# A decoder block on one core: the first half's projection without the norm's factor, its differences, squares and gate in other places

## The chip, the cores and the metric

The kernel runs on one core of a Trainium2 chip. The metric is the device time of one execution in microseconds (us). In the texts PE is TensorE (matmuls), ACT is ScalarE, DVE is VectorE, POOL is GpSimd and SP is SyncE, from whose queue all loads and stores are issued. Each engine runs its own instructions in a fixed order, and waits when an operand or a buffer is not ready.

## What is computed

One layer on x of 2048 positions by 1024 channels. The parts that matter here:

```python
h = rmsnorm(x, norm1_g[l])          # y = x * rsqrt(mean(x*x) + eps), times g
proj = h @ w_in[l]
p_q, p_k, p_v, p_g, p_a, c_b, c_c, c_h = jnp.split(proj, splits, axis=-1)
q, k, v = p_q * 64 ** -0.5, p_k, p_v              # 4 heads
log_a = jax.nn.log_sigmoid(p_a @ w_gate_up[l] + b_gate[l]) / 16
o = gla_chunked(q, k, v, log_a)                   # chunks, state carried on
o = rmsnorm(o, gla_norm_g[l]) * jax.nn.silu(p_g)
u = c_c * c_h
o_conv = c_b * causal_depthwise_conv(u, conv_w[l])
x = x + jnp.concatenate([o, o_conv], axis=-1) @ w_out[l]
h2 = rmsnorm(x, norm2_g[l])
x = x + (silu(h2 @ w_ffn_gate[l]) * (h2 @ w_ffn_up[l])) @ w_ffn_down[l]
return rmsnorm(x, norm_f_g)
```

The norm's factor rsqrt(mean(x*x) + eps) is one number for each position. It commutes with the projection, so proj is the same number times (x * g) @ w_in.

## The kernel before

The positions are worked on in two halves of 1024, each half as two column blocks j of 512. Channels lie on the 128 partitions, in 8 tiles k for each j. Products are made in fp32r with operands split into a high and a low half: split (L152) lets ACT write the high half and DVE the difference, and a product of 128 channels takes three matmuls (high by high, high by low, low by high; product_step, L386).

The input projection of a half is 12 units u = 0 to 11 (in_proj, L626): k and q (0, 1), v (2, 3), the swish gate (4, 5), then twice c_c, c_h, c_b (6 to 8, 9 to 11). A unit's weights are four quarters of 128x512. Units 2 to 11 are made by seven products in Strassen's manner (PRODUCTS, L34) with weight sums S1 to S4 made on POOL (L374 to L381) and input differences T1 to T4; each of the seven is 12 matmuls. The products accumulate in PSUM banks named mm; some are copied by ACT (c11, c22, c12; L413) before a later product goes on in the same bank, others are added by DVE (L417). Units 0 and 1 of the first half are made without differences, with 96 matmuls each.

The first half starts like this. first_loads (L496) brings rows of x, the first unit's weight quarters (raw) and the transposed input tiles (h). ACT squares the rows (L494), rows_rstd (L479) makes the factor and spreads it over the partitions by four transposes on PE (L488). build_first (L288) then multiplies each input tile by norm weight and factor on DVE (L520), splits it, and issues its six matmuls (L312 to L314). The differences T1, T2, T3 on POOL (L325) are issued behind that, T4 behind unit 1.

The other work is in generators that a tick, after each product, moves on by a step (background, L205; every tick while hurry is set): the gate's weights, the row statistics of the second half, gate (L577: a_ps from the projection's 16 columns, then for four parts z, and in forget_gate Abs, Exp, Ln on ACT and a running sum on DVE), and h1_ahead (L546), which prepares the second half's operands and stores them (si). gla_half (L680) joins after unit 5. The order in which each engine gets its instructions is then made by the program's scheduler, which may put later work first; issue_after holds an instruction behind a given one on the same engine. ACT's function tables are loaded where the order of its functions needs it (ACT_TABLE_LOAD).

Of the kernel before, what the change touches and what calls it, by code (L numbers as in the profile page):

```python
# [51 lines left out]
def tile_hymba_block(ctx, tc, x, xt, win, wa, wgu, wout, wffn, wdown, wdown_first, small, out):  # L52
# [97 lines left out]
    last_hi, raw_loads = [], []  # L150

    def split(src, hi, lo):  # L152
        last_hi[:] = [act.activation(hi, src, AF.Copy)]  # L153
        return dve.tensor_tensor(lo, src, hi.bitcast(F32), ALU.subtract)  # L154
# [71 lines left out]

    def pause(n):
        for _ in range(n):
            yield
# [58 lines left out]
    def build_first(quad, w):  # L288
# [3 lines left out]
        h, o = {}, {}  # L292
        quarters = ("A11", "A12"), ("A21", "A22")
        los = []
        for j in range(2):
            for r in range(2):
                o[r, j] = bank()
            for k in range(KD):
                with ExitStack() as stack:
                    if len(los) > 1:  # L300
                        stack.enter_context(tc.issue_after(los[-2].ins))
                    h[k, j] = quad(k, j)
# [12 lines left out]
            if j == 0:  # L315
                rbs[1] = rows_rstd(squares[1])

        def differences(wanted):
            for n, y, a, b in (
                ("T1", (0, 0), (0, 1), (0, 0)), ("T2", (0, 0), (4, 1), (0, 0)),  # L320
                ("T3", (0, 1), (4, 1), (0, 1)), ("T4", (0, 0), (4, 0), (0, 0)),
            ):
                for k in range(4 if n in wanted else 0):
                    yy, aa, bb = [h[k + dk, j] for dk, j in (y, a, b)]
                    pool.tensor_tensor(yy[:], aa[:], bb[:], ALU.subtract)  # L325
                    ops[n].append(split_op(yy[:]))

        return ops, [(r, j, o[r, j], True) for j in range(2) for r in range(2)], differences

    def plain_unit(src, ops):  # L330

        raw = raw_weights(src)
# [14 lines left out]
    def weight_quarter(src):  # L347
# [10 lines left out]
        split(src, h[:, 0, :], h[:, 1, :])  # L358
        return h
# [35 lines left out]
    def unit(src, ops, into=None, raw=None, onto=None):  # L395
# [13 lines left out]
        def copied(name, o, at):  # L409
# [3 lines left out]
            act.activation(t[:], o[:], AF.Copy)  # L413
# [43 lines left out]
    def row_stats(b):  # L457
# [11 lines left out]
        for t in range(PT):  # L469
# [3 lines left out]
            for e, xn in enumerate(xs):  # L473
                act.activation(xn[:], xn[:], AF.Square, accum_out=ssq[:, t, e : e + 1])
# [4 lines left out]
    def rows_rstd(ssq):  # L479

        v, l, y0 = [mtiny.tile([P, PT], F32, name=n, tag=n) for n in ("msq", "rl", "ry")]
# [9 lines left out]
    rbs, raws, first_weights, last_load, rows, squares = {}, {}, {}, [], {}, {}  # L491
# [4 lines left out]
    def first_loads():  # L496

        raw = rawp.tile([P, 4, PB], F32, name="raw", tag="raw")
        for b in range(2):
# [6 lines left out]
            for k in range(KD):  # L506
                if b == 0 and k % 4 == 0:
                    for i in ((0, 3), (1, 2))[k // 4]:
                        raw_loads.append(load(raw[:, i, :], win[0][:, i, :]))
                h = bt("h") if b else tt("h")  # L510
                raws[b, k] = h
                last_load[:] = [load(h[:], xt[b, :, k, :])]
        for t in range(PT):
            row_squares(0, t)
        rbs[0] = rows_rstd(squares[0])
        for n, i in (("A11", 0), ("A21", 3), ("A12", 1), ("A22", 2)):
            first_weights[n] = weight_quarter(raw[:, i, :])
# [20 lines left out]
    def build_h():  # L538


        def quad(k, j):
            return scaled(col(C_G1 + k), rbs[j], raws[j, k])

        return build_first(quad, first_weights)
# [32 lines left out]
    def gate(half, ops):  # L577
# [15 lines left out]
        act.activation(a_sb[:], a[:], AF.Copy)  # L593
# [32 lines left out]
    def in_proj(half, ops, first=None, differences=None):  # L626
        def units():
            for u in range(12):
# [7 lines left out]
                if half == 0 and u == 1:  # L636
                    del ops["B12"]
                    differences(("T4",))
# [664 lines left out]
```

## Time and profile before

| | us |
|---|---|
| median of 3 runs (range) | 2085.23 (2084.04 to 2087.19) |
| the profiled execution | 2085.32 |
| its span, first to last instruction | 2083.6 |
| PE busy in the span | 2026.7 (97%) |
| DVE, ACT, POOL busy | 1429.0, 965.2, 882.6 |

The span is counted from the first instruction; all starts are from there. In a timeline a line has start and duration in us, engine, line of the kernel, operation, what is written and read, and in brackets the idle time before and what ended it. A matmul's duration there runs longer than its share, since matmuls overlap; the step between two starts tells the pace. A line of waits has the waiting engine, what it waited for, the total in us, how many times, and the longest.

### The profile page before, as it was taken

How to read it: one execution, taken by the hardware profiler on the slowest of the kernel's cores; microseconds unless marked ns; L12 is line 12 of the kernel's file. 1: busy time of each engine (PE TensorE's matmuls, PEld its weight loads, DVE VectorE, ACT ScalarE, POOL GpSimd, SP SyncE). 2: the span in 40 equal slices, each digit the busy share in tenths (PEclk: the TensorE clock that was granted, in tenths of full speed). 3: DMA queues.
4: the chain of work that ended last, by engine and by line, in shares of the span. 5: the costliest groups of instructions: out<-in, count | busy, mean ns of one | idle time of the engine just before them, and what ended most of it. 6: DMA issues, size and time to landing. Idle time of an engine off the chain costs nothing.

```text
span 2083.6 us, 26960 instructions
## 1 busy us (share of the span) xinstructions
PE 2026.7 (97%) x9175; PEld 1651.2 (79%) x9175; DVE 1429.0 (69%) x2057; ACT 965.2 (46%) x1918; POOL 882.6 (42%) x642
## 2 busy tenths in 40 slices
PE   5999999999999999999999999999999999999997
PEld 4778888887888887778888878887888888878886
DVE  7669786549754696787887566654776776666665
ACT  6455455656543245554555442223455444443234
POOL 3427322222102364555555434533655534534545
PEclk9999999999999999999999999999999999999999
DMA  7349495424586882654654587689454465398763
GB/s 277 126 152 313 145 342 160 152 96 137 182 304 206 331 295 96 234 218 175 237 222 163 211 344 275 237 328 361 167 185 159 177 227 202 136 354 318 288 263 121
DMA packets 190395, 464.45 MB, mean 223 GB/s; under 512 B 19952, under 2 KB 67248, under 8 KB 180656
## 3 DMA queue, kind: packets, MB, share of 16 engines
q1 hardware_dynamic: 190256, 462.72, 61.5%
q8 instruction: 72, 1.18, 0.2%
q14 instruction: 67, 0.55, 0.1%
HBM read 297.49 MB, written 165.15 MB: 222 GB/s over the span
## 4 chain that ended last, share of the span: by engine, by line
PE 79%; DVE 6%; DMA 3%; issue 2%; POOL 1%; ACT 1%; SPq 0%; DVEq 0%; POOLq 0%; ACTq 0%
PE mm L391 23%; PE mm L393 23%; PE mm L392 22%; PE mm L824 3%; PE mm L825 2%; PE mm L827 2%; DVE wq L154 2%; DVE so L154 1%; DMA raw<-in_wffn_dram 1%; DMA shT<-so 1%; PE o_ps L748 1%; PE o_ps L750 1%; DMA op<-sa_T 1%; PE sc L724 0%; POOL t L927 0%
## 5 line engine op out<-in xcount | busy, mean ns | idle before, releaser
L391 PE MATMUL mm<-op,wq 128*128 128x512 f32 x2511 | 982.1, 393 | 10.8 <-ACT c L413 5.0
L392 PE MATMUL mm<-op,wq 128*128 128x512 f32 x2511 | 977.3, 389 | 0.0
L393 PE MATMUL mm<-op,wq 128*128 128x512 f32 x2511 | 964.8, 390 | 10.4 <-DVE wq L154 10.2
L154 DVE TENSOR_TENSOR wq<-raw,wq 128x512 fp32r<-128x512 f32 (+2 forms) x626 | 503.0, 810 | 230.7 <-ACT wq L153 228.6
L153 ACT ACTIVATE wq<-raw 128x512 fp32r<-128x512 f32 (+2 forms) x626 | 363.8, 587 | 590.2 <-PE mm L393 456.2
L391 PEld LDWEIGHTS mm<-op,wq 128*128 128x128 f32 x2511 | 472.4, 188 | 122.7 <-ACT c L413 8.6
L393 PEld LDWEIGHTS mm<-op,wq 128*128 128x128 f32 x2511 | 472.5, 188 | 116.7 <-DVE wq L154 18.8
L392 PEld LDWEIGHTS mm<-op,wq 128*128 128x128 f32 x2511 | 472.7, 188 | 96.4 <-issue 1.2
L376 POOL TENSOR_TENSOR raw<-s,raw 128x512 f32<-128x512 f32 (+2 forms) x97 | 127.1, 1310 | 473.4 <-DVE wq L154 446.9
L417 DVE TENSOR_TENSOR y<-mm,y 128x512 f32<-128x512 f32 x185 | 127.2, 689 | 131.5 <-PE mm L393 131.2
L374 POOL TENSOR_TENSOR s<-raw 128x512 f32<-128x512 f32 (+2 forms) x97 | 128.0, 1320 | 205.3 <-DMA raw<-in_wffn_dram 101.4
L381 POOL TENSOR_TENSOR raw<-raw 128x512 f32<-128x512 f32 (+2 forms) x97 | 124.9, 1288 | 164.7 <-DVE wq L154 157.6
L417 DVE TENSOR_TENSOR c<-mm,c 128x512 f32<-128x512 f32 x198 | 135.3, 683 | 64.9 <-PE mm L393 63.6
L806 POOL TENSOR_TENSOR ssx<-ssx,q 128x512 f32<-128x512 f32 x52 | 76.1, 1478 | 161.6 <-ACT q L805 161.5
L375 POOL TENSOR_TENSOR raw<-raw 128x512 f32<-128x512 f32 (+2 forms) x97 | 135.8, 1400 | 5.3
L413 ACT ACTIVATE c<-mm 128x512 f32<-128x512 f32 x198 | 114.9, 587 | 17.3 <-PE mm L393 15.8
L154 DVE TENSOR_TENSOR so<-t,so 128x512 fp32r<-128x512 f32 x100 | 89.1, 896 | 25.2 <-ACT so L153 24.7
L153 ACT ACTIVATE wq<-s 128x512 fp32r<-128x512 f32 (+2 forms) x97 | 56.7, 585 | 95.9 <-PE mm L393 89.0
L824 PE MATMUL mm<-op,wq 128*128 128x512 f32 x256 | 100.9, 395 | 0.0
L825 PE MATMUL mm<-op,wq 128*128 128x512 f32 x256 | 99.8, 390 | 0.0
L154 DVE TENSOR_TENSOR wq<-s,wq 128x512 fp32r<-128x512 f32 (+2 forms) x97 | 81.1, 836 | 9.8 <-ACT wq L153 9.2
L153 ACT ACTIVATE so<-t 128x512 fp32r<-128x512 f32 x100 | 62.5, 627 | 41.6 <-DMA sa_B<-so 17.8
(188 smaller groups left out, 1847.9 us busy)
## 6 DMA issues: line engine op xcount, KB each, us to landing
raw<-in_wffn_dram SPq DMA_DIRECT2D x44, 1024.0 KB, 5.6
sa_T<-so SPq DMA_DIRECT2D x88, 512.0 KB, 5.3
op<-sa_T SPq DMA_DIRECT2D x88, 512.0 KB, 9.6
sa_B<-so SPq DMA_DIRECT2D x69, 512.0 KB, 3.4
op<-sa_B SPq DMA_DIRECT2D x69, 512.0 KB, 9.6
raw<-in_win_dram SPq DMA_DIRECT2D x23, 1024.0 KB, 5.5
raw<-in_wdown_dram SPq DMA_DIRECT2D x24, 768.0 KB, 6.2
sx<-y SPq DMA_DIRECT2D x48, 256.0 KB, 3.0
```

The lines of the kernel that those rows point to most:

```text
L153: last_hi[:] = [act.activation(hi, src, AF.Copy)]
L154: return dve.tensor_tensor(lo, src, hi.bitcast(F32), ALU.subtract)
L374: pool.tensor_tensor(s1, a21, a22, ALU.add)
L375: pool.tensor_tensor(a21, a11, a21, ALU.subtract)
L376: pool.tensor_tensor(a11, s1, a11, ALU.subtract)
L381: pool.tensor_tensor(a12, a12, a11, ALU.subtract)
L391: pe.matmul(o[:, s], wh, xh, start=first and k == 0, stop=False, skip_group_check=True)
L392: pe.matmul(o[:, s], wh, xl, start=False, stop=False, skip_group_check=True)
L393: return pe.matmul(o[:, s], wl, xh, start=False, stop=k == n - 1, skip_group_check=True)
L417: dve.tensor_tensor(t[:], o[:], t[:], ALU.add)
L824: pe.matmul(o[e, j][:], wh, m[:, 0, :], start=k == 0, stop=False)
L825: pe.matmul(o[e, j][:], wh, m[:, 1, :], start=False, stop=False)
```

## The change

The first half's operands are now the input times the norm's weight alone. ACT writes the high half of that product (scale=g), DVE the low half in one scalar_tensor_tensor, and POOL writes the product itself back to h for the differences. Unit 0's weights come by quarters in between, and the loads of weights and input tiles come ahead of the rows of x. The factor is made later, in the background (first_factors), and is put in behind the projection: on v as its square at the positions (positions), on the head norm, on the swish gate, on c_c as its square (factors2) and on the convolution's result by products on POOL (on DVE for the bank still in PSUM), and on the gate's 16 columns. opening issues T1, T2, T3 and the eight row squares at ticks of unit 1. 18 small matmuls on ones stand at PE's start. The gate's generator stands behind the row statistics and eight steps of h1.

```diff
+                g = col(C_G1 + k)
+                if j == 0 and k in (0, 3, 4):
+                    turn(*{0: ("A11", 0), 3: ("A12", 1), 4: ("A22", 2)}[k])
                 x = opp.tile([P, 2, PB], F32R, name="op", tag="op")
-                los.append(split(h[k, j][:], x[:, 0, :], x[:, 1, :]))
-                if j == 0 and k >= PT:
-                    row_squares(1, k - PT)
+                with tc.issue_after(order[-1].ins):
+                    order.append(act.activation(x[:, 0, :], h[k, j][:], AF.Copy, scale=g))
+                if (k, j) == (0, 0):
+                    turn("A21", 3)
+                dve.scalar_tensor_tensor(
+                    x[:, 1, :], h[k, j][:], g, x[:, 0, :].bitcast(F32), ALU.mult, ALU.subtract
+                )
+                pool.tensor_scalar(h[k, j][:], h[k, j][:], g, 1.0, ALU.mult, ALU.mult)
...
+    def opening(differences):
+        def some_squares(b, t):
+            with tc.issue_after(last_weight[0].ins):
+                row_squares(b, t)
+                row_squares(b, t + 1)
+
+        differences("T1", range(4))
+        some_squares(0, 0)
+        yield
+        some_squares(0, 2)
+        yield
+        for i in range(2):
+            differences("T2", range(2 * i, 2 * i + 2))
+            yield
+        for i in range(2):
+            some_squares(1, 2 * i)
+            differences("T3", range(2 * i, 2 * i + 2))
+            yield
+        yield from pause(2)
+
+    def first_factors():
+        for b in range(2):
...
+            with tc.issue_after(last_lo[0].ins):
+                act.activation(factors[b][:], rows_rstd(squares[b], f)[:], AF.Copy)
+                dve.tensor_tensor(f2[:], f[:], f[:], ALU.mult)
...
+    def factored(c, in_psum, f):
+
+        s = tt("n") if in_psum else c
+        (dve if in_psum else pool).tensor_tensor(s[:], c[:], f[:], ALU.mult)
+        return s
...
-        act.activation(a_sb[:], a[:], AF.Copy)
+        if half:
+            act.activation(a_sb[:], a[:], AF.Copy)
+        else:
+            for j in range(2):
+                r = slice(32 * j, 32 * j + 32)
+                dve.tensor_tensor(a_sb[r, :], a[r, :], factors[j][r, :], ALU.mult)
...
+                if half == 0 and u in (4, 5, 6, 9):
+                    c, p = factored(c, p, f[j]), False
...
+                    if half == 0:
+                        pool.tensor_tensor(y[:], y[:], factors[j][:], ALU.mult)
...
+            act.activation(v[:], v_ps[:], AF.Copy, scale=positions[b][1][:, t : t + 1])
...
+    warm = bank("warm")
+    for _ in range(18):
+        pe.matmul(warm[:, 0:P], ones[:], ones[:], start=True, stop=True)
     act.preload_act_table_set("natural_log_exp_and_others")
-    first_loads()
+    raw, second = first_loads()
...
     background.extend(
         [
-            gate_weights(), pause(9), row_stats(2), row_stats(3), gate(0, ops), unhurried(),
-            h1_ahead(),
+            opening(differences), gate_weights(), first_factors(), pause(3), row_stats(2),
+            row_stats(3), begun(h1, 8), gate(0, ops), unhurried(), h1,
         ]
     )
```

Three places of the new order follow. The first is DVE at the start of the program, from its first weight split on; first as it was before (msq, rl are the factor's small tiles, rb_ps its spread in PSUM, wq weights, op operands, h input tiles).

```order
L482 TENSOR_SCALAR msq<-ssq 128x4
L154 TENSOR_TENSOR wq<-raw,wq 128x512 x2
L163 TENSOR_TENSOR rl<-ry 128x4
L164 SCALAR_TENSOR_TENSOR rl<-rl,msq 128x4
L165 SCALAR_TENSOR_TENSOR msq<-rl,ry 128x4
L487 COPY rep<-msq 128x128 x4
L520 SCALAR_TENSOR_TENSOR h<-h,sml,rb_ps 128x512 x2
```

The same place of DVE in the changed order (L320 is the new low half).

```order
L154 TENSOR_TENSOR wq<-raw,wq 128x512
L320 SCALAR_TENSOR_TENSOR op<-h,sml,op 128x512
L154 TENSOR_TENSOR wq<-raw,wq 128x512
L320 SCALAR_TENSOR_TENSOR op<-h,sml,op 128x512 x2
L154 TENSOR_TENSOR wq<-raw,wq 128x512
L320 SCALAR_TENSOR_TENSOR op<-h,sml,op 128x512
L154 TENSOR_TENSOR wq<-raw,wq 128x512
```

The factor's operations are gone from there, and low halves of operands (20 operations for 16 tiles and four quarters) take their place. The second place is POOL right behind its constants, in the changed order; before, the differences L325 were its first work there.

```order
L323 TENSOR_SCALAR h<-h,sml 128x512 x10
L341 TENSOR_TENSOR h<-h 128x512
L323 TENSOR_SCALAR h<-h,sml 128x512
L341 TENSOR_TENSOR h<-h 128x512
L323 TENSOR_SCALAR h<-h,sml 128x512 x3
L341 TENSOR_TENSOR h<-h 128x512
L323 TENSOR_SCALAR h<-h,sml 128x512 x2
L341 TENSOR_TENSOR h<-h 128x512 x5
L391 TENSOR_TENSOR s_935<-raw 128x512
L341 TENSOR_TENSOR h<-h 128x512 x4
```

POOL now has a product for each input tile, with T1 between; s_935 is the weight sum s1 of unit 2, ahead of T2. The third place is ACT in the gate. Before, with the tiles g1 of the gate's parts, between unit 3 and 4:

```order
L442 ACTIVATE c11_1375<-mm_1149 128x512
L153 ACTIVATE wq_1393<-raw_1378 128x512
L610 ACTIVATE g1_1356<-z_1354,sml_99 128x512
L612 ACTIVATE g1_1356<-g1_1356 128x512
L613 ACTIVATE g1_1356<-g1_1356,ones_92 128x512
L153 ACTIVATE wq_1396<-raw_1378 128x512
L413 ACTIVATE c11_1437<-mm_1406 128x512
L610 ACTIVATE g1_1421<-z_1419,sml_99 128x512
L620 ACTIVATE em_1351<-g1_1356 128x4
L612 ACTIVATE g1_1421<-g1_1421 128x512
L613 ACTIVATE g1_1421<-g1_1421,ones_92 128x512
```

In the changed order the gate stands between unit 5 (raw_1531, c22_1590, c12_1613) and unit 6 (raw_1780, bank mm_1808). L660 is Abs, L662 Exp, L663 Ln, L469 silu.

```order
L469 ACTIVATE c22_1590<-c22_1590 128x512
L660 ACTIVATE g1_1682<-z_1680,sml_99 128x512
L153 ACTIVATE wq_1792<-raw_1780 128x512
L662 ACT_TABLE_LOAD
L662 ACTIVATE g1_1682<-g1_1682 128x512
L660 ACTIVATE g1_1713<-z_1711,sml_99 128x512
L663 ACT_TABLE_LOAD
L663 ACTIVATE g1_1682<-g1_1682,ones_92 128x512
L662 ACT_TABLE_LOAD
L662 ACTIVATE g1_1713<-g1_1713 128x512
L660 ACTIVATE g1_1747<-z_1745,sml_99 128x512
L469 ACT_TABLE_LOAD
```

It goes on from there (em and el are small results of the gate, wq_1795 and wq_1798 weights A12 and S3 of unit 6):

```order
L663 ACT_TABLE_LOAD
L663 ACTIVATE g1_1713<-g1_1713,ones_92 128x512
L662 ACT_TABLE_LOAD
L662 ACTIVATE g1_1747<-g1_1747 128x512
L670 ACTIVATE em_1677<-g1_1682 128x4
L663 ACT_TABLE_LOAD
L663 ACTIVATE g1_1747<-g1_1747,ones_92 128x512
L672 ACT_TABLE_LOAD
L672 ACTIVATE el_1679<-g2_1683 128x4
L153 ACTIVATE wq_1795<-raw_1780 128x512
L153 ACTIVATE wq_1798<-raw_1780 128x512
L430 ACTIVATE c11_1839<-mm_1808 128x512
```

Where Abs, Exp and Ln stood without table loads between them, eight loads now stand between the first Abs and the copy c11_1839. The same stretch of PE in the changed order, at the end of unit 6's second product (S1, bank mm_1841):

```order
L410 MATMUL mm_1841<-op_769,wq_1789 128x512
L408 MATMUL mm_1870<-op_603,wq_1795 128x512
L409 MATMUL mm_1870<-op_603,wq_1795 128x512
L408 MATMUL mm_1808<-op_804,wq_1792 128x512
L409 MATMUL mm_1808<-op_804,wq_1792 128x512
L410 MATMUL mm_1808<-op_804,wq_1792 128x512
```

PE takes A12's weights wq_1795 and then goes on in bank mm_1808, which c11_1839 reads.

More of the change, by code (lines that the diff above doesn't have):

```diff
@@ L225, in unhurried, with begun @@
         yield
+    def begun(work, n):
+        for _ in range(n):
+            next(work)
+            yield
     def pause(n):
@@ L489, in rows_rstd @@
         return rb_ps
[L491 removed]
+    rbs, raws, positions, rows, squares, factors, factors2 = {}, {}, {}, {}, {}, {}, {}
     def row_squares(b, t):
@@ L505, in first_loads @@
                 load(xr[:], x[r0 : r0 + P, :])
[L506 to L517, printed above, removed]
+        return raw, second
     def scaled(g, rb, h):
@@ L636, in units @@
                 if half == 0 and u == 1:
                     del ops["B12"]
[L638 removed]
+                    differences("T4", range(4))
                 yield us
         units = units()
[L642 to L645 removed]
+        for u, (dst, i0) in enumerate(((s_kq, 0), (s_kq, 2), (s_v, 0), (s_v, 2))):
+            for r, j, c, p in values(u):
@@ L646, in in_proj @@
                 store(dst[2 * half + j][i0 + r][:], settled(c, p)[:])
         for i0 in (0, 2):
-            for r, j, c, p in next(units):
+            for r, j, c, p in values(4 + i0 // 2):
                 store(s_g[2 * half + j][i0 + r][:], silu(c, p)[:])
         background.append(gla_half(half))
+        if half == 0:
+            for j in range(2):
+                factors2[j] = tiny.tile([P, PB], F32, name=f"rr{j}", tag=f"ssx{j}", bufs=1)
+                act.activation(factors2[j][:], factors[j][:], AF.Square)
```

119 lines of the change are left out of this document (69 added, 50 removed).

## Prediction

> **What bounds the kernel now.** I read the page first, then the waits of PE, then the timeline around the waits. The profiled execution took 2085.32 us (span 2083.6 and 1.7 around it), 0.1 us above the median of the runs, 2085.23; the sum is made against it.
>
> ```profile
> PE 2026.7 (97%) x9175; PEld 1651.2 (79%) x9175; DVE 1429.0 (69%) x2057; ACT 965.2 (46%) x1918; POOL 882.6 (42%) x642
> ...
> PE rb_ps L488 <- DVE rep L487: 14.4, 2, 14.2
> PE mm L312 <- ACT op L153: 4.1, 2, 2.6
> PE mm L313 <- DVE op L154: 3.2, 2, 2.6
> ```
>
> PE is busy for 97%, so only PE's idle and slow stretches can be won. The waits (us in total, times, longest) put 21.7 us of them into the first projection unit: it waits for the norm's factor (L488), then for operands.
>
> ```profile
> 18.24 1.22 PE L312 MATMUL mm<-op,wq 128*128 128x512 f32 x2 [2.58 <-ACT op L153]
> ...
> 65.43 0.80 PE L393 MATMUL mm<-op,wq 128*128 128x512 f32 x1 [2.06 <-DVE wq L154]
> 66.02 0.63 PE L391 MATMUL mm<-op,wq 128*128 128x512 f32 x1
> ...
> 70.71 0.63 PE L393 MATMUL mm<-op,wq 128*128 128x512 f32 x1
> ...
> 71.48 0.39 PE L392 MATMUL mm<-op,wq 128*128 128x512 f32 x1
> ...
> 78.07 0.39 PE L393 MATMUL mm<-op,wq 128*128 128x512 f32 x1
> 78.30 0.39 PE L391 MATMUL mm<-op,wq 128*128 128x512 f32 x1
> ```
>
> The first product of unit 0 starts at 18.24. From 71.48 to 78.07 there are 29 steps of 0.227 us (warm); from 66.02 to 70.71 11 steps of 0.427 us: after the waits 13 products ran slow and lost 13 x 0.2 = 2.6 us. Counted in PE's order, the row at 78.30 is the first product of unit 2. Units 0 and 1 hold 192 products, 43.6 us warm, so before 78.30 PE has lost 34.7 us.
>
> **The start.** The input now goes straight from its load to the operands: no row squares, no factor, no L520 between. Ahead of the first input tile stand a small load and two weight quarters of 256 KB.
>
> ```profile
> 4.83 1.06 ACT L494 ACTIVATE xr<-xr 128x1024 f32<-128x1024 f32 x1 [2.75 <-DMA xr<-in_x_dram]
> ...
> 6.88 1.06 ACT L494 ACTIVATE xr<-xr 128x1024 f32<-128x1024 f32 x1 [0.90 <-DMA xr<-in_x_dram]
> ...
> 10.56 0.63 ACT L153 ACTIVATE wq<-raw 128x512 fp32r<-128x512 f32 x1
> ...
> 11.23 0.69 DVE L154 TENSOR_TENSOR wq<-raw,wq 128x512 fp32r<-128x512 f32 x1 [0.39 <-ACT wq L153]
> ...
> DMA packets 4318, 9.64 MB, mean 321 GB/s; under 512 B 656, under 2 KB 720, under 8 KB 4304
> ```
>
> Today's first loads of 512 KB are there at 4.83 and 6.88. The first input tile ends 0.81 MB, which lies at 6.0 between them. ACT's high half (0.63) makes 6.6, the second weight's high half 7.3 and its low half on DVE 8.0; so column block 0 is done at about 8.4. The other 15 blocks of unit 0 take 6 x 0.227 = 1.36 each, 20.4, and unit 1 takes 21.8: unit 2 would start at 50.6 if PE alone set the pace.
>
> Does supply keep up? The last input tile ends 6.3 MB; at the mean of the first 30 us (321 GB/s) and the same lag that is 22 to 24 us, and block 15 starts at 27. Loads hide. DVE and POOL are closer:
>
> ```profile
> 1.08 0.29 POOL masks.py:199 TENSOR_SCALAR_AFFINE_SELECT ident<-ident 128x128 f32<-128x128 f32 x1
> ...
> 1.40 0.41 POOL L80 TENSOR_SCALAR_AFFINE_SELECT mask<-mask 128x256 f32<-128x256 f32 x1
> ...
> 33.77 5.93 POOL L325 TENSOR_TENSOR h<-h 128x512 f32<-128x512 f32 x4 [31.96 <-DVE h L520]
> ...
> 37.88 3.12 DVE L154 TENSOR_TENSOR wa_sb<-wa,wa_sb 128x64 fp32r<-128x64 f32 x3
> ...
> L325 POOL TENSOR_TENSOR h<-h x1: 1282/1282/1282, 33.8 to 33.8; 128x512 f32<-128x512 f32 x1
> ...
> L269 POOL TENSOR_TENSOR t<-h 128x512 f32<-128x512 f32 x2 | 4.2, 2086 | 16.7 <-DVE h L520 16.7
> ```
>
> While POOL ran its differences back to back, three tiny DVE operations took 1.04 us each: a DVE operation that reads two SBUF operands waits for a POOL one, and they take turns. The new L320 reads two, and behind each comes the new POOL product L323 (16 of them). No row shows L323. Below, the selects: 0.12 us for 128 columns more, hence 0.65 for 512; above, the longest two-operand POOL row, 2.09. I take 0.65, since with one operand it is nearest to the selects. Then 20 DVE operations of 0.69 and 16 of 0.65 in turns are 24.2 us from 6.6 on, 30.8 against PE's 28.8: 2.0 more. The 18 products on ones run while PE would idle and cost nothing; whether they keep the clock up is open, 0 to 2.6, taken as 1.4. Unit 2 starts at 54.0: **-24.3 us**.
>
> **Units 1 to 5.** T1's splits, eight row squares (1.06 and an accumulator read each) and the weights of unit 1's second half stand in one row on ACT. The squares' loads moved behind the input's on SP; 4.2 MB more at the same rate land at 34 to 36, and T2 on POOL stands behind the sum s1 of unit 2's weights, which lands after them. POOL's 16 products and four T1 (10.4 + 5.1) and the turns put T1 at 33; four squares (5.0) and a copy and a split (1.2) later the weights for unit 1's second half are ready at 40, with DVE's half at 41, and PE wants them at 41 to 43; unit 2's A11 is likewise ready within 1 us of its need. I put **+2.0** (0 to 5). The factors' transposes stay 8 and come later: 0. That silu now waits for a POOL product holds up the weight splits behind it on ACT by some 2.5 us; PE has three products (8.2) until it wants them.
>
> **The gate's place.** It moves from units 3 and 4 to units 5 and 6, behind the first silu.
>
> ```profile
> 125.00 1.12 PE L601 MATMUL z<-a_sb,wgu_sb 32*128 32x512 f32 x2
> ...
> 125.60 0.62 ACT L153 ACTIVATE wq<-raw 128x512 fp32r<-128x512 f32 x1
> 126.16 0.69 ACT L610 ACTIVATE g<-z,sml 128x512 f32<-128x512 f32 x1
> 126.88 0.63 ACT L612 ACTIVATE g<-g 128x512 f32<-128x512 f32 x1
> 127.54 0.72 ACT L613 ACTIVATE g<-g,ones 128x512 f32<-128x512 f32 x1
> ...
> 145.22 0.21 ACT L620 ACTIVATE em<-g 128x4 f32<-128x4 f32 x1 [1.20 <-DVE g L617]
> 145.45 1.28 ACT L452 ACT_TABLE_LOAD   x1
> 146.75 0.63 ACT L452 ACTIVATE c<-c 128x512 f32<-128x512 f32 x1
> ...
> PE mm L393 <- DVE wq L154: 2.1, 1, 2.1
> PE mm L391 <- ACT c L413: 0.9, 1, 0.9
> ```
>
> Today Exp (L612) and Ln (L613) follow each other with no load of tables between; one load takes 1.30 from start to next start. The last two rows are PE's waits from 140 to 180, where the gate and the input's second half are made today. In the changed order eight loads stand between the gate's first Abs and the copy c11_1839, because silu's tables are in and Exp and Ln then fetch theirs in turn. Let t be the end of unit 5's S3 product. PE makes z at t + 2.4. Silu of c22 waits for DVE's sum and POOL's product, so ACT is free at t + 3.0. Then: 8 loads 10.4, three Exp and three Ln 4.0, three Abs 1.9, one silu 0.5, two short ones 0.3, three weight splits 1.6, the copy 0.5: 19.2, to t + 22.2. PE up to there has 45 products of 0.227 and four z of 0.53 (half of 1.12, as they overlap) and two products of A12: t + 12.8, and its next product writes over what c11_1839 still has to read. It waits 9.4 us, and after that runs slow as at 65.43, 2.6: **+12.0**. Bounds: 0 if something holds PE back as long anyway, 17 if DVE's scans behind the gate add up too. Today's 3.0 of waits from 140 to 180 belong to the old place and go: **-3.0**.
>
> The Trainium skill, "ScalarE: Activation LUTs", section What ACT_TABLE_LOAD costs, has 1.28 us for the load and some 1.38 more of draining for each switch. The trace does not agree on the second part: ACT's row before the load ends at 145.43, and 146.75 comes 1.30 after its start. By the page the estimate would be 8 x 1.38 = 11 us more, 2083.
>
> **The rest.** POOL gets 20 products more (12 for units 4, 5, 6 and 9, 8 behind the convolution), 26 to 42 us at 1.28 to 2.09, over some 150 us in which it has about 30% free:
>
> ```profile
> 160.00:180.00 20.00, 19.18 (x84) 15.88 (x85) 17.51 (x21) 10.97 (x20) 13.78 (x9) 1.00 0.97 327
> 180.00:200.00 20.00, 20.00 (x90) 16.56 (x89) 19.77 (x21) 11.21 (x20) 13.87 (x9) 1.00 0.91 328
> ```
>
> POOL (13.8 of 20) stays under PE, so I put 0; without that cover each is 1.3 on PE's path. Two factor copies and two squares on ACT (2.4), four products on DVE, the scales on activations already there, and eight h1 steps with their loads and stores ahead of the gate: beside PE. Behind the first tenth or so PE's order is the old one, as are its waits. Sum: -24.3 + 2.0 + 12.0 - 3.0 = -13.3, so 2085.3 becomes **2072**.
>
> **Rivals.**
> - Slower: POOL's L323 costs as much as its longest row. Turns of 0.69 + 2.09 = 2.78 instead of 1.36 for each of 16 blocks: 22.7 us more, 2095. It decides once a turn passes 1.36 + 13.3/16 = 2.19, L323 1.5 us. For it: POOL rows of that length exist; against: they read two operands. Chance 0.06. Halfway, at 1.28 as the lone difference, a turn is 1.97: 9.8 more, 2082, 0.08.
> - The gate's tables cost PE nothing, since ACT gets ahead or PE is held elsewhere: 2060. For it: ACT is busy 46%. Against: PE wants the copy inside the chain. 0.10.
> - Every table switch empties ACT for as long again: 8 x 1.28, 2082. Against: the row at 146.75. 0.04. The Trainium skill's rule cited above would be this case.
> - The start does not move, because weights and input come no earlier than today: PE starts by loads, at 18. Then -24.3 shrinks to the -8 or so of the waits behind the start: 2088. Against: 4.83 and 6.88. 0.02.
> - My sum: 0.70, with its own range 2065 to 2079 (the parts' bounds of 0 to 5, 0 to 2.6 and a wait of 7 to 14).
>
> A measurement of this kernel tells about 0.2%, 4.2 us, from no change. 2061 to 2083 leaves out the slow POOL, the late start and half of the free gate. Faster takes the sum, the free gate and part of the halfway case: 0.84; the same 0.09; slower 0.07.
>
> **What would show it.** In the profile after: PE's first product (but for the ones) near 6.6 and no wait for rb_ps ahead of it; unit 2 near 54; L323 near 0.65; ACT_TABLE_LOAD at L662 and L663 in turns between 120 and 160, and one PE wait there of about 9 us on ACT (weight wq or copy c), with slow products behind it; the waits behind 200 as before. Wrong would be: L323 above 1.5, several waits of PE in units 1 to 3, or no wait at the gate.

## The result, and the profile after

The changed kernel takes 2099.93 us (median; 2097.7 to 2102.52) against 2084.64 us (2083.71 to 2087.19) of the kernel before measured beside it: a ratio of 1.0072, 95% interval 1.006 to 1.0084. It is 15 us slower, clear of the noise, where 13 us faster was forecast, and outside the range (2061 to 2083). The profiled execution's span is 2099.4 us.

PE starts early, as forecast. The timeline of PE after shows the products on ones (the 18 products are 36 matmuls there, of which the row has the last 20), then the first product of unit 0, and the product that opens unit 2:

```profile
4.69 3.35 PE L1231 MATMUL warm<-ones 128*128 128x128 f32 x20
7.80 0.77 PE L329 MATMUL mm<-op,wq 128*128 128x512 f32 x2
...
52.72 0.39 PE L408 MATMUL mm<-op,wq 128*128 128x512 f32 x1
```

Unit 2 starts at 52.7, not at 78.3: 25.6 us won. By the end of unit 9 the same product of PE's order comes 11.9 us *later* than before. The table gives the time of each unit in the profiled executions, from the last product ahead of it to its own last product, so that a start in the table is 0.2 us ahead of the unit's first product (a unit is 84 products, 19.0 us warm; where the gate's products stand, 8 to 10 us more). e1 to e11 are experiments below; they stand here so that the rows can be compared.

| us | before | after | e1 | e2 | e3 | e4 | e5 | e11 |
|---|---|---|---|---|---|---|---|---|
| unit 2 starts | 78.1 | 52.5 | 52.4 | 53.0 | 52.3 | 55.1 | 52.5 | 52.9 |
| unit 2 | 19.3 | 29.4 | 34.5 | 29.4 | 29.4 | 24.2 | 29.4 | 29.4 |
| unit 3 | 27.3 (gate) | 20.2 | 25.2 (gate) | 20.2 | 20.2 | 20.2 | 20.2 | 20.6 |
| unit 4 | 24.1 | 21.1 | 21.6 | 21.1 | 21.0 | 22.2 | 21.1 | 31.1 (gate) |
| unit 5 | 22.9 | 29.1 (gate) | 22.1 | 29.1 (gate) | 19.6 | 29.1 (gate) | 21.3 | 25.0 |
| unit 6 | 19.0 | 33.4 | 19.5 | 30.6 | 32.1 (gate) | 34.8 | 31.2 (gate) | 21.0 |
| unit 7 | 19.0 | 23.6 | 25.3 | 22.1 | 27.3 | 24.7 | 24.4 | 21.8 |
| unit 8 | 19.5 | 29.4 | 26.6 | 24.1 | 27.7 | 28.3 | 24.4 | 24.4 |
| unit 9 | 19.2 | 21.6 | 22.0 | 20.7 | 21.7 | 21.6 | 19.8 | 21.1 |
| unit 9 ends | 248.4 | 260.3 | 249.1 | 250.3 | 251.2 | 260.2 | 244.2 | 247.4 |

The lead, and 11.9 us more, goes in three places: 10.1 us in unit 2 (7.1 of waits, the rest in slow products behind them), 10.5 in units 3 to 6 (103.8 against 93.3), 16.9 in units 7 to 9 (74.6 against 57.7). The waits of PE after (us in total, times, longest), from 40 to 80, 140 to 200 and 200 to 260, name the engine. Before, PE had no wait at all from 200 to 260.

```profile
PE mm L410 <- DVE wq L154: 6.1, 2, 5.0
PE mm L408 <- ACT c L430: 1.0, 1, 1.0
...
PE mm L408 <- ACT wq L153: 7.6, 1, 7.6
PE mm L410 <- DVE wq L154: 6.2, 4, 1.8
...
PE mm L410 <- DVE wq L154: 5.7, 3, 4.3
PE mm L408 <- ACT c L430: 2.9, 2, 1.6
```

In these stretches PE waits 18.0 us for DVE, always for the low halves of weights (L154), and 11.8 us for ACT (0.3 of them in a row not shown), of which 7.6 are the one wait at the gate. The stretches of 20 us after (span; busy PE, PEld, DVE, ACT, POOL; clock; DMA) show DVE full:

```profile
180.00:200.00 20.00, 14.55 (x60) 10.76 (x59) 20.00 (x25) 6.11 (x12) 16.51 (x11) 1.00 0.78 258
200.00:220.00 20.00, 15.96 (x69) 12.46 (x67) 19.08 (x22) 7.98 (x18) 12.90 (x9) 1.00 0.70 234
220.00:240.00 20.00, 16.97 (x63) 12.74 (x64) 19.81 (x23) 7.96 (x17) 13.03 (x8) 0.91 0.65 211
```

A full DVE alone is not the loss. Before, it was as full from 180 to 220 (the prediction has the row from 180 to 200, the next one is below), and PE ran through. What differs is how much DVE has to do for the same products: 51.9 us in units 7 and 8, against 38.2 before.

```profile
200.00:220.00 20.00, 19.96 (x88) 16.06 (x87) 19.96 (x26) 9.62 (x23) 10.99 (x7) 1.00 0.76 237
```

The same view, cut where unit 2 starts and where unit 9 ends, first of the kernel before, then after:

```profile
0.00:78.30 78.30, 53.23 (x201) 40.49 (x201) 61.07 (x95) 48.72 (x110) 32.77 (x28) 0.96 0.69 241
78.30:248.40 170.10, 167.02 (x721) 133.08 (x720) 127.09 (x178) 82.07 (x151) 72.86 (x48) 1.00 0.58 198
```

```profile
0.00:52.50 52.50, 51.13 (x228) 42.39 (x229) 37.20 (x43) 34.48 (x63) 43.59 (x39) 1.00 0.76 272
52.50:260.30 207.80, 176.41 (x729) 135.76 (x728) 158.17 (x220) 106.83 (x208) 103.28 (x68) 0.97 0.56 184
```

When unit 2 started, DVE had 61.1 us of work behind it before, and 37.2 after. PE came 25.6 us earlier, and 23.9 us of DVE's work was not yet done. Up to the end of unit 9 DVE now has 158.2 us to do instead of 127.1: those 23.9 and 7.2 more in all (195.4 against 188.2), while POOL's sum rose from 105.6 to 146.9. Theory C of the experiments reads it so: from unit 2 to unit 8 PE's lead lives as long as DVE keeps up, and DVE, with the turns that it takes with POOL, does not.

### The profile page after: what moved, and what is told of

Same layout as the page of the kernel before. It is cut to its first block, busy times and chain, and to the rows that moved or that the text cites. A ratio compares the mean times of both kernels' runs of the same rounds, so it can differ in the third digit from the quotient of the medians.

```text
span 2099.4 us, 27112 instructions
## 1 busy us (share of the span) xinstructions
PE 2036.2 (97%) x9211; PEld 1656.8 (79%) x9211; DVE 1439.4 (69%) x2057; ACT 979.3 (47%) x1926; POOL 932.3 (44%) x678
## 4 chain that ended last, share of the span: by engine, by line
PE 77%; DVE 8%; DMA 6%; ACT 3%; issue 3%; POOL 2%; SPq 0%; DVEq 0%; POOLq 0%; ACTq 0%
PE mm L408 22%; PE mm L410 22%; PE mm L409 22%; DVE wq L154 2%; PE mm L889 2%; PE mm L890 2%; PE mm L892 2%; DMA op<-shT 1%; DVE so L154 1%; PE a_ps L633 1%; DVE op L154 1%; POOL h L323 1%; DMA sa_T<-so 1%; DMA h<-in_xt_dram 1%; DVE c L434 1%
## 5 line engine op out<-in xcount | busy, mean ns | idle before, releaser
L154 DVE TENSOR_TENSOR wq<-raw,wq 128x512 fp32r<-128x512 f32 (+2 forms) x626 | 507.1, 816 | 223.4 <-ACT wq L153 221.8
L154 DVE TENSOR_TENSOR so<-t,so 128x512 fp32r<-128x512 f32 x100 | 88.3, 889 | 23.8 <-ACT so L153 23.5
L154 DVE TENSOR_TENSOR wq<-s,wq 128x512 fp32r<-128x512 f32 (+2 forms) x97 | 81.6, 841 | 9.9 <-ACT wq L153 9.3
```

Of the source, the lines that this page charges most:

```text
L154: last_lo[:] = [dve.tensor_tensor(lo, src, hi.bitcast(F32), ALU.subtract)]
```

## The experiments

Before them two theories stood. **A:** POOL's 20 new products with the factor hold up DVE. **B:** the gate, in its new place, puts its work on DVE and its table loads on ACT into the full stretch. **C**, above, came after the first four. The ratios are to the kernel before, measured beside each; the changed kernel has 1.0072.

**e1, the gate ahead of the row statistics.**

```diff
-            opening(differences), gate_weights(), first_factors(), pause(3), row_stats(2),
-            row_stats(3), begun(h1, 8), gate(0, ops), unhurried(), h1,
+            opening(differences), gate_weights(), first_factors(), pause(3), gate(0, ops),
+            row_stats(2), row_stats(3), begun(h1, 8), unhurried(), h1,
```

> The changed kernel with the gate put ahead of the row statistics of the second half, so that it is made in units 2 and 3, where no silu has been issued yet and Exp and Ln find their tables. Theory A (POOL's 20 new products hold up DVE, which is full in units 7 to 9): the gate's stall goes, 12 to 14 us, units 7 to 9 still lose about 17, so 2086 to 2088. Theory B (the gate's own work, 16 scans and 16 other operations on DVE, some 20 us, now falls into the stretch in which DVE is full, and holds up the low halves of the weights there): both losses go, 2070 to 2075. If neither the gate's tables nor its DVE work cost anything: 2098 to 2101.

Measured: 2089.09 us, 1.0027 (1.0017 to 1.0037). Units 5 and 6 fall from 62.5 to 41.6 us, units 2 and 3 pay 10.1 of it, and units 7 to 9 still lose 16 (73.8). The time is 1 us above A's range and far from B's: the gate's DVE work is no longer near units 7 to 9, and they are as slow as before the edit.

**e2, no products with the factor.**

```diff
-                if half == 0 and u in (4, 5, 6, 9):
-                    c, p = factored(c, p, f[j]), False
...
-                    if half == 0:
-                        pool.tensor_tensor(y[:], y[:], factors[j][:], ALU.mult)
```

> The changed kernel with the products with the row factor left out behind units 4, 5, 6 and 9 (12 on POOL, 4 on DVE) and behind the convolution (8 on POOL): these outputs miss the factor. The gate stays where the change put it. Theory A: the 17 us that units 7 to 9 lose go, the gate's stall stays: 2082 to 2085. Theory B: POOL has room for them and they cost next to nothing: 2096 to 2100.

Measured: 2090.32 us, 1.0032 (1.0019 to 1.0045), between the two. Units 7 to 9 fall from 74.6 to 67.0 us: the products are worth half of the loss there, not all of it. The stretches of units 7 and 8 of e2 show DVE still full in unit 8:

```profile
183.36:205.50 22.14, 20.08 (x86) 15.40 (x84) 20.94 (x27) 9.24 (x20) 14.37 (x10) 1.00 0.86 281
205.50:229.62 24.12, 21.54 (x85) 16.71 (x84) 24.12 (x31) 10.85 (x22) 11.88 (x8) 0.93 0.70 243
```

**e3, the gate four steps later, its tables loaded once.**

```diff
+        if not half:
+            with tc.issue_after(last_silu[0].ins):
+                last_exp[:] = [act.preload_act_table_set("natural_log_exp_and_others")]
...
-            row_stats(3), begun(h1, 8), gate(0, ops), unhurried(), h1,
+            row_stats(3), begun(h1, 12), gate(0, ops), unhurried(), h1,
```

The first Abs of the gate is issued after that load.

> The changed kernel with the gate four steps later (12 steps of h1 ahead of it instead of 8), behind unit 5's silus, and with one load of the logarithm's and exponential's tables behind the last silu, so that Exp and Ln fetch none. The gate's DVE work stays in the full stretch, and POOL's products stay. If the eight table loads make the stall of 7.6 us on weight wq and the slow products behind it, the time falls by 9 to 14, to 2086 to 2091 (theory A and the gate's term of the prediction). If the stall comes from the gate's work on DVE as such (theory B), it only moves into unit 6: 2096 to 2102.

Measured: 2087.57 us, 1.0013 (1.0000 to 1.0026), inside the first forecast. Units 5 and 6 fall by 10.8 (51.7 against 62.5). With one load of tables units 3 to 6 take 92.9 us, as long as before the change (93.3): the alternating tables cost what the gate lost there. The edit also moves the gate by four steps; what that alone does is not told apart. Units 7 and 8 get slower by 2.0 (55.0 against 53.0).

**e4, no product with the norm's weight on POOL in the first unit.**

```diff
-                pool.tensor_scalar(h[k, j][:], h[k, j][:], g, 1.0, ALU.mult, ALU.mult)
```

> The changed kernel without the 16 POOL products of the input with the norm's weight in the first unit (L323): the differences T1 to T4 are made of the bare input, so they miss the norm's weight. This takes 16 x 1.1 to 1.4 us from POOL ahead of T1. If the loss of 10 us in unit 2 (6.1 us of waiting for the first low half of its weights) comes from POOL being late with T1 to T4 and DVE taking turns with it, unit 2 starts without that wait: 2088 to 2092. If it comes from the order on ACT or DVE whatever POOL does: 2097 to 2101.

Measured: 2097.76 us, 1.0067 (1.0045 to 1.0090): no difference from the changed kernel that can be told. Unit 2 is 5.2 us shorter as the first theory said, but it starts 2.6 later, and by the end of unit 6 the rest is gone: 185.6 against 185.7. A gain ahead of the gate was absorbed behind it.

**e5, the edits of e2 and e3 together** (both diffs above, with nothing else changed).

> The two edits of e2 and e3 together: the gate four steps later with its tables loaded once, and the products with the row factor left out behind units 4, 5, 6 and 9 and behind the convolution (so these outputs miss the factor). Theory A and the tables as two separate losses: 12.3 and 9.6 add up, 2099.9 - 21.9 = 2078, and units 7 to 9 take about 60 us together. Theory C (DVE is the bound from unit 6 to unit 9, and what matters is how much of its work, with the turns it takes with POOL, is still to do when unit 6 begins; the step 'PE's order is the old one' is right and beside the point): the sums do not add, since either edit leaves DVE full; units 7 to 9 stay above 66 us together, 2081 to 2086.

Measured: 2081.41 us, 0.9983 (0.9968 to 0.9998). The time does not decide between the forecasts: e2's and e3's gains would add up to a ratio of 0.9973, inside the interval. It is the one version below the kernel before; but it leaves products out. The units speak for theory C: 7 to 9 take 68.6 us, not 60. With neither the products nor the tables, 11 us of loss stay there; some 2 of them may be the gate's work on DVE, which e3's edit moves towards these units.

**e6 and e8, h1 made whole in the idle stretch.** e6 is e3 with

```diff
+            opening(differences), gate_weights(), first_factors(), row_stats(2), row_stats(3),
+            h1, gate(0, ops), unhurried(),
```

> The changed kernel with e3's tables for the gate, and the second half's input (h1) made whole ahead of the gate, at one step a product, right behind its row statistics and without the pause of three: in units 3 to 7, where DVE idles 7 to 13 us of every 20, and not in units 7 and 8. POOL's products with the factor all stay. Theory C: units 7 and 8 find DVE less full; against e3 (2087.6) the time falls by 5 to 12, to 2076 to 2082. Theory A (POOL's products themselves hold DVE up in units 7 to 9, by 8 to 10 us): no change there, 2086 to 2089.

and e8 has the gate first, without e3's load of tables:

```diff
+            opening(differences), gate_weights(), first_factors(), row_stats(2), row_stats(3),
+            gate(0, ops), h1, unhurried(),
```

> The changed kernel with row statistics, gate and h1 in this order, without the pause of three, h1 at one step a product to its end. The gate is issued in units 3 and 4, ahead of most silus (seven table loads fewer), and its DVE work and h1's come before the convolution. POOL's products with the factor all stay. Theory C: both losses of the changed kernel shrink, and its early start is kept in good part: 2068 to 2078. Theory A: the gate's stall goes, units 7 to 9 still lose their 16: 2086 to 2089, as in e1.

Measured: 2105.26 us, 1.0094 (1.0064 to 1.0123), and 2104.53 us, 1.0090 (1.0068 to 1.0112). No gain, against all forecasts; by the ratios both are some 4 us above the changed kernel, but the intervals overlap. In e8 unit 8 ends at 226.9, 12 us earlier than in the changed kernel; what follows gives it back. The first scores of the attention in the changed kernel, and in e8:

```profile
287.85 0.71 PE L783 MATMUL sc<-kq 64*128 64x128 f32 x8
```

```profile
214.78 0.71 PE L783 MATMUL sc<-kq 64*128 64x128 f32 x8 [0.81 <-DVE kq L773]
```

The attention is the next in the background's row, so it came forward with h1.

**e11, e8 with the attention held back.**

```diff
-            gate(0, ops), h1, unhurried(),
+            gate(0, ops), h1, unhurried(), pause(12),
```

> e8 with twelve empty steps behind h1, so that the attention's chunks (gla) begin again at the end of unit 11, as in the changed kernel, and not in unit 8. If e8 gave its gain back because gla came forward into units 8 to 10, where DVE still had the convolution: the end of unit 8 stays near 225 and the rest runs as in the kernel before, 2078 to 2084. If h1 at one step a product is what costs (DVE full in units 5 and 6 instead of 7 and 8): 2090 and more.

Measured: 2086.11 us, 1.0012 (1.0002 to 1.0021), 18 us below e8: the attention's place was e8's loss. The time is 2 us above the first forecast and below the second. The stretch from unit 2 to the end of unit 9 in e11:

```profile
52.90:247.40 194.50, 175.11 (x730) 135.44 (x729) 163.45 (x221) 97.64 (x201) 106.70 (x68) 0.97 0.57 196
```

DVE does 163.5 us of work in 194.5 us, where the changed kernel does 158.2 in 207.8: it is busy for 84% instead of 76%. Unit 9 ends at 247.4, 13 us earlier than in the changed kernel and 1 us earlier than in the kernel before. Of the 13 us, 7.3 are won in units 7 to 9, where 10 of h1's operations stand in units 7 and 8 instead of 17, and 6.0 in units 3 to 6, where the gate now stands ahead of most silus and tables are loaded 3 times instead of 10. No run separates these two gains. More than the 13 us is not won: PE's early start is lost here too.

**e10, one product on ones instead of 18.**

```diff
-    for _ in range(18):
+    for _ in range(1):
```

> The changed kernel with one product on ones at the start instead of 18. If the 18 keep the clock up at the start, the first dozen products of unit 0 run at 0.43 instead of 0.23 us and unit 0 ends 2 to 3 us later; since DVE or the gate sets the time behind it (theory C), the end of the kernel does not move: 2098 to 2102. If PE is the bound from the start on: 2102 to 2104.

Measured: 2099.41 us, 1.0067 (1.0046 to 1.0089), no difference at the end. At the start the ones make a difference: without them PE's first dozen products run 0.43 us apart up to about 12.6, with them 0.23 us apart wherever they do not wait:

```profile
9.17 0.63 PE L331 MATMUL mm<-op,wq 128*128 128x512 f32 x1
9.60 0.63 PE L330 MATMUL mm<-op,wq 128*128 128x512 f32 x1
...
13.58 0.39 PE L331 MATMUL mm<-op,wq 128*128 128x512 f32 x1
13.81 0.39 PE L330 MATMUL mm<-op,wq 128*128 128x512 f32 x1
```

Unit 0 ends at 31.7 instead of 30.3. Those 1.4 us reach unit 2 as 1.0 and the end as nothing.

**e12, the convolution's product with the factor one unit later** (on e3).

```diff
-                    if half == 0:
-                        pool.tensor_tensor(y[:], y[:], factors[j][:], ALU.mult)
...
                 dve.tensor_tensor(y[:], c[:], y[:], ALU.mult)
+                if half == 0:
+                    pool.tensor_tensor(y[:], y[:], factors[j][:], ALU.mult)
```

> e3 (gate behind unit 5's silus, tables once) with the convolution's product with the factor on POOL moved behind DVE's last product of each block, so that it comes in units 8 and 11 and not in 7 and 10. The output is the same product. If the turns that DVE takes with these POOL products in unit 7 are what holds it up, units 7 and 8 (27.3 and 27.7 us in e3) fall by 3 to 6 together: 2082 to 2085. If DVE is full there whichever POOL product stands beside it: 2086 to 2089.

Measured: 2089.74 us, 1.0028 (1.0018 to 1.0038), no gain over e3, just above the second forecast. Unit 8 falls from 27.7 to 24.8, unit 9 rises from 21.7 to 27.4: the loss moved with the products.

**e13, DVE's work taken away, POOL's left.**

```diff
-            split(h[:], hi[:], lo[:])
-            for e, y in enumerate((hi, lo)):
+            act.activation(hi[:], h[:], AF.Copy)
+            for e, y in enumerate((hi, hi)):
```

> The changed kernel with the 16 low halves of h1's operands left out on DVE (the high half is stored in their place, so the second half's products miss the low halves). Everything of POOL, the gate and its tables stays. Of the 16, ten fall into units 7 and 8, 13.8 us of DVE. If DVE's sum of work is the bound there (theory C), units 7 and 8 shrink by 8 to 14 and the time falls to 2086 to 2092. If only the turns with the new POOL products matter (theory A): 2095 to 2100.

Measured: 2091.49 us, 1.0042 (1.0027 to 1.0057), 6 us below the changed kernel by the ratios: inside theory C's range and outside A's. Units 7 to 9 fall from 74.6 to 68.7 us, nearly as much as without the products with the factor (67.0). But units 7 and 8 shrink by 4.1 us, and theory C had forecast 8 to 14 for the 13.8 us taken from DVE. PE now waits there 3.8 us for copies by ACT (c) and 2.6 for DVE, so DVE's sum of work is not the only bound in these units.

**e14 and e15, unit 2's first low half.** The timeline of DVE after shows what stands ahead of it (the row at 57.56 is the weight PE waits for):

```profile
49.64 2.71 DVE L154 TENSOR_TENSOR wa_sb<-wa,wa_sb 128x64 fp32r<-128x64 f32 x3
52.27 0.23 DVE L531 TENSOR_SCALAR f<-ssq 128x4 f32<-128x4 f32 x2
52.42 5.22 DVE L154 TENSOR_TENSOR op<-h,op 128x512 fp32r<-128x512 f32 x5
57.56 0.68 DVE L154 TENSOR_TENSOR wq<-raw,wq 128x512 fp32r<-128x512 f32 x1
```

e14 is e11 with three moves (begun also draws two steps at a time, as in e16's diff below):

```diff
-                    differences("T4", range(4))
+                    behind_first.append(lambda: differences("T4", range(4)))
...
         w = {"A11": weight_quarter(a11)}
+        if behind_first:
+            behind_first.pop()()
...
-        yield from pause(2)
...
+            opening(differences), first_factors(), row_stats(2), row_stats(3), gate_weights(),
+            gate(0, ops), begun(h1, 4), h1, unhurried(), pause(16),
```

> e11 with three moves ahead of unit 4: T4's differences and splits behind the split of unit 2's first weight instead of ahead of it, the gate's weight splits behind the row statistics, and the opening's two empty steps and the steps of h1 drawn together (two at a time for the first eight). The arithmetic is the same. If unit 2 loses its 10 us because DVE has the splits of T3 and T4 and of the gate's weights ahead of the unit's first low half, the wait of 5.0 us there shrinks to 2 or less and unit 2 takes 23 to 26 us instead of 29.4; if that is kept to the end, 2078 to 2082. If DVE's sum of work up to unit 8 is the bound (theory C), what unit 2 gains is lost again by unit 8 as in e4, 2084 to 2088.

Measured: 2095.59 us, 1.0046 (1.0031 to 1.0062), a miss of both forecasts, by a new wait. Its wait for the factor from 40 to 70:

```profile
PE rb_ps L539 <- DVE rep L538: 12.3, 2, 10.9
```

Without the two empty steps, and with the gate's weights moved behind them, the factor's transposes came earlier in PE's order than DVE could make their input, and PE stood behind them for 10.9 us: in the table's count unit 2 starts at 64.3. e15 therefore is e11 with T3 and T4 behind the first weight, and nothing else.

```diff
-            differences("T3", range(2 * i, 2 * i + 2))
...
-                    differences("T4", range(4))
+                    behind_first.append(lambda: [differences(n, range(4)) for n in ("T3", "T4")])
```

> e11 with the differences T3 and T4 and their splits issued behind the split of unit 2's first weight; nothing else is moved (the factors' transposes keep their place, other than in e14). On DVE three splits (1.05 us each) that stood ahead of that weight's low half then stand behind it. If the 5.0 us wait of unit 2 is made by the splits ahead on DVE, it falls by about 3 and unit 2 takes 26 to 27 us instead of 29.4. By theory C little of that reaches the end, since DVE is full from unit 4 on and its work is the same: 2084 to 2087. If PE's lead is kept, 2081 to 2084.

Measured: 2086.54 us, 1.0014 (1.0005 to 1.0024), e11's time. Its waits for DVE from 40 to 80:

```profile
PE mm L412 <- DVE wq L154: 5.6, 3, 2.2
```

The two waits of the changed kernel (6.1 us) became three (5.6 us), and unit 2 takes the same 29.4 us: with three splits moved behind the first low half, the next one was late. That fits the amount of DVE's work there as the limit, and not the order of these splits.

**e16 and e17, h1 two steps at a time behind the gate; the statistics drawn together.** e16 is e15 with

```diff
             next(work)
+            next(work)
             yield
...
-            gate(0, ops), h1, unhurried(), pause(12),
+            gate(0, ops), begun(h1, 4), h1, unhurried(), pause(16),
```

> e15 with the first eight steps of h1, behind the gate, drawn two at a time, and the empty steps behind h1 at sixteen, so that gla keeps its place. By theory C only work that DVE does earlier helps: h1 comes forward by four products, some 5 us of DVE, at a place (units 4 and 5) where DVE is already full, so nothing: 2084 to 2088. If h1 is held back by its steps and not by DVE: 2079 to 2083.

e17 is e11 with both row statistics advanced in each step, so that gate and h1 come earlier (both_stats draws a step of each):

```diff
-            opening(differences), gate_weights(), first_factors(), row_stats(2), row_stats(3),
-            gate(0, ops), h1, unhurried(), pause(12),
+            opening(differences), gate_weights(), first_factors(), both_stats(),
+            gate(0, ops), h1, unhurried(), pause(17),
```

> e11 with the two row statistics of the second half drawn together, two steps a product, so that the gate and h1 follow some 25 products of PE (6 us) earlier, into unit 3, where DVE idles 10 of 20 us in e11. DVE's work is the same. By theory C this is what helps, since the stretch in which DVE is full begins earlier: 2080 to 2084. If the input rows, their loads or buffers hold the statistics back, nothing moves: 2085 to 2088.

Measured: 2086.81 us, 1.0012 (1.0001 to 1.0023), and 2086.51 us, 1.0009 (1.0000 to 1.0017). Neither moved. In e17 the gate's products stand in unit 3, unit 4 then takes 26.5 us, and unit 9 ends at 247.9. Theory C forecast a gain for e17 that did not come; why an earlier gate did not help is not settled. What stands is that four orders of the same work (e1, e11, e15, e17) all end unit 9 between 246.9 and 249.1, where the kernel before has 248.4.

## Why the prediction was wrong, point by point

| term of the sum | forecast | measured |
|---|---|---|
| the start | -24.3 | -25.6 |
| units 1 to 5 | +2.0 | +10.1, all in unit 2 |
| the gate's place, with the old waits | +12.0 - 3.0 | +10.5 (units 3 to 6) |
| the rest, units 7 to 9 | 0 | +16.9 |
| the rest, behind unit 9 | 0 | +4.3 |

The measured column is counted in PE's order up to the last product of this kind (16.2 us in all); the two profiled executions differ by 15.8.

- **The start** was right to 1.3 us, in part because its terms balance: the first product came at 7.80, later than the sum had it (8.4 less 1.36, 7.0), while the 1.4 us for a slow clock did not fall due, and units 0 and 1 lost 1.3 us and not 2.0 against the warm pace. The turns of DVE and POOL were also near their price. The timelines of DVE and of POOL after:

```profile
13.30 14.07 DVE L320 SCALAR_TENSOR_TENSOR op<-h,sml,op 128x512 fp32r<-128x512 f32 x12
```

```profile
8.38 3.85 POOL L323 TENSOR_SCALAR h<-h,sml 128x512 f32<-128x512 f32 x3 [6.57 <-DVE op L320]
...
14.58 5.54 POOL L323 TENSOR_SCALAR h<-h,sml 128x512 f32<-128x512 f32 x5 [0.64 <-DVE op L320]
...
31.75 1.36 POOL L323 TENSOR_SCALAR h<-h,sml 128x512 f32<-128x512 f32 x2
```

  A turn is 14.07/12 = 1.17 us (forecast 1.36). Beside L320, L323's rows read 1.1 to 1.3 us, not 0.65. The last row, which starts while DVE stands idle, has 0.68 each, the price that was taken; so the longer rows seem to hold the wait for DVE. The rival of a slow POOL, decided at 1.5, did not occur.
- **The gate** was right in mechanism and size. Its timeline on ACT after shows the tables in turns:

```profile
160.78 1.28 ACT L662 ACT_TABLE_LOAD   x1
162.07 0.63 ACT L662 ACTIVATE g<-g 128x512 f32<-128x512 f32 x1
162.61 0.19 ACT L670 ACTIVATE em<-g 128x4 f32<-128x4 f32 x1
162.82 1.28 ACT L663 ACT_TABLE_LOAD   x1
164.12 0.72 ACT L663 ACTIVATE g<-g,ones 128x512 f32<-128x512 f32 x1
164.85 1.28 ACT L672 ACT_TABLE_LOAD   x1
```

  PE's wait there is 7.6 us (forecast 9.4), the clock 0.83 from 160 to 180, and e3 got 10.8 us back with one load of the tables (and the gate four steps later). The second part of the rule of the Trainium skill, "ScalarE: Activation LUTs", section What ACT_TABLE_LOAD costs, 1.38 us of draining for each switch, is again not seen: 162.61 plus 0.19 is 162.80, the load starts at 162.82, and the next activation 1.30 later. The Trainium skill, "ScalarE: Activation LUTs", section Table sets: the hidden batching unit, says that logarithm and exponential share a set; e3 shows what that is worth when the set is asked for by name.
- **Units 1 to 5** were right in kind (T1 to T4 and unit 2's first weight come late) and mis-sized: 2.0 for 10.1. The working followed POOL and ACT into unit 2, and not DVE, which had 23.9 us of work left over. e15 shows that moving splits behind the weight only moves the wait.
- **The rest, 0, is the step that failed.** It reads: "POOL (13.8 of 20) stays under PE, so I put 0; without that cover each is 1.3 on PE's path". The cover was looked for on the wrong engine. In the rows quoted there DVE stood at 17.51 and 19.77 of 20, and the turns make POOL's time DVE's time. In units 7 and 8 DVE's 12 low halves of raw weights took 1260 ns each after, against 986 before and 0.68 us alone; and of h1's operations (lo, and h with rb_ps) 17 with 18.8 us stand there, against 8 with 8.0 us. In groups by line, before and after:

```profile
L154 DVE TENSOR_TENSOR wq<-raw,wq 128x512 fp32r<-128x512 f32 x12 | 11.8, 986 | 0.1
...
L154 DVE TENSOR_TENSOR lo<-h,hi 128x512 fp32r<-128x512 f32 x2 | 3.0, 1478 | 0.0
L520 DVE SCALAR_TENSOR_TENSOR h<-h,sml,rb_ps 128x512 f32<-128x512 f32 x4 | 2.9, 734 | 0.0
...
L154 DVE TENSOR_TENSOR lo<-t,hi 128x512 fp32r<-128x512 f32 x2 | 2.1, 1068 | 0.0
```

```profile
L154 DVE TENSOR_TENSOR wq<-raw,wq 128x512 fp32r<-128x512 f32 x12 | 15.0, 1260 | 0.0
L154 DVE TENSOR_TENSOR lo<-h,hi 128x512 fp32r<-128x512 f32 x5 | 7.3, 1454 | 0.0
L154 DVE TENSOR_TENSOR lo<-t,hi 128x512 fp32r<-128x512 f32 x5 | 6.5, 1308 | 0.6 <-ACT hi L153 0.6
...
L567 DVE SCALAR_TENSOR_TENSOR h<-h,sml,rb_ps 128x512 f32<-128x512 f32 x7 | 5.0, 736 | 0.3 <-DMA h<-in_xt_dram 0.3
```

  The products themselves are half of it: 7.7 of 16.9 (e2). The other half is not settled. It fits h1's operations, which crowd there: without their low halves units 7 to 9 take 5.9 us less (e13), with h1 further forward 7.3 less (e11). Whether they come late because DVE's work from the start was still to do, or because the changed program places them there, no run shows. "PE's order is the old one, as are its waits" was right in the order and wrong in the waits.
- The forecast had no rival in which an early PE runs into another engine's arrears. Of its cases slower than before, one hung on the price of a single instruction (L323) and the other on late loads.
- The 4.3 us behind unit 9 were not traced. Of them 3.1 come up to the 1500th product, where the attention of the first half runs.

## What to carry to other kernels

Winning time at the start for the engine that bounds is worth only what the next engine has in reserve: sum the work of each other engine from the new start to the point where it last idles, before and after. Here PE's lead (25.6 us) was about what DVE had still to do (23.9), and the lead was eaten; e17 shows that such a sum does not explain every order. A free share on one engine is no cover when its instructions take turns with an engine that is already full; look at the full one's row, and count what it has to do for the same products. Where the background is a row of tasks, moving one forward also moves what stands behind it.

## What the runs showed of the hardware

- DVE and POOL take turns also where POOL reads one tensor only: L320 has a pitch of 1.17 us with L323 beside it, where a DVE operation on two operands alone takes 0.68 (the row at 57.56 above). The Trainium skill, "SBUF — State Buffer", section SBUF: two separate sides, has a DVE operation with two SBUF inputs and a GpSimd operation that reads SBUF exclude each other for a whole instruction; the pitch agrees with such turns, by estimate (1.17 less 0.68) with about 0.5 us of POOL on top of DVE's own in each.
- Taking 10 of DVE's operations out of units 7 and 8 (e13) and taking out the products with the factor, 20 on POOL and 4 on DVE in the whole half (e2), shortened units 7 to 9 by 5.9 and 7.7 us.
- Exp and Ln behind a silu loaded tables in turns (1.28 us each, 8 between the gate's first Abs and the copy c11), though one set, asked for by name, serves both (e3).
